# A decoder trunk layer on one core: two PSUM banks for attention scores and transposes, and branch gates kept as plain tanh

## The chip, the cores and the metric

The kernel runs on one core of a Trainium2 chip. A core has a matrix engine (TensorE, PE in the profile, with PEld for its weight loads), three engines for elementwise work (VectorE or DVE, ScalarE or ACT, GpSimd or POOL), a queue that mostly issues transfers (SyncE or SP), and 16 DMA engines. Matmul results land in PSUM, which has eight banks; ACT and DVE read them from there. Each engine works through its own instructions in order, and semaphores tie the engines together.

The metric is the device time of one execution in microseconds (us), lower is better. The kernel before was timed three times: 2133.55, 2133.91 and 2136.91 us, median 2133.91.

## What is computed

One inference step of one decoder layer, for a prompt of 1024 rows and 8 single-row samples, all in fp32, with a model width of 1024. In short:

```
h   = RMSNorm(x) * (1 + scale1) + shift1            # scale, shift, gate from silu(c) @ w_mod
z   = h @ w_in                                      # columns: delta rule, attention q k v, gates ga gb
y_a = GatedRMSNorm(GatedDeltaRule(conv4(q, k, v))) @ w_gdn_out
y_b = SlidingWindowSinkAttention(q, k, v) @ w_swa_out     # window 128, 16 heads, 4 key heads
x   = x + gate1 * (sigmoid(ga) * y_a + sigmoid(gb) * y_b) @ w_o
h2  = RMSNorm(x) * (1 + scale2) + shift2
x   = x + gate2 * (silu(conv3(h2 @ w_gate)) * (h2 @ w_up)) @ w_down
y   = RMSNorm(x)
```

Beside y the kernel returns the updated states: the delta rule's matrices, the last rows of both convolutions, and the last 128 keys and values.

## The kernel before, in words

**Matmuls.** Every projection multiplies split operands: a matrix is stored as a high part, rounded to the fast fp32r format, and a low part, the rest. `split` (L127) makes both: ACT copies to the high part (L129), DVE subtracts it from the source (L130). `mm3` (L177) adds three products, high x high, high x low, low x high (L180 to L182). The 1032 columns (rows of x) are worked on in three parts of 384, 384 and 264 (`PARTS`), or in four quarters of 256, 256, 260 and 260 (`QUARTERS`). A projection of one tile of 128 output channels over one part is 24 matmuls into one PSUM bank of the pool "mm", which an evacuation function then empties.

**Stages.** Setup: `modulation` (L250) computes the conditioning into tile "sc" and its transposes, `norm_part` (L278) spreads the row norms through "sc", `turn_part` (L304) transposes x through "pt" and "pv". Attention (L473): keys, queries and values are projected; four groups (one key head, four query heads) of eight blocks (128 queries) follow. Delta rule: eight heads are prepared, inverted and scanned in chunks. Branches (L1289): the two output projections with their gates. Then the output projection, the second norm, and the feed-forward part.

**An attention block** (L628). Two halves of two heads each: four matmuls write the scores into "sc" (L639, L640); ACT copies the older key block's scores to tile E (L643), DVE copies the newer block's where they are causal (L645). The softmax runs on E: row maximum on DVE (L647), exponentials with sums on ACT (L655), scaling by the reciprocal on ACT and DVE (L660, L662). PE transposes the four heads into "pt", DVE masks them on the way out (L667, L670), PE multiplies with the values into "pv" (L676, L678), ACT copies the result (L679).

**PSUM during setup and attention.** The pool q2 holds "sc", "pt" and "pv", beside two banks "mm" (pmm) and one more (pmf). How many buffers a tag has is decided in `t`, which keeps a table: the first number given for a pool and a tag stays (a `setdefault`). `modulation` and `conditioning` are the first to ask for "sc" and "pt" and name no number, which leaves the pool's own, one; `attention_block` asks later, with bufs=2. Before them, a line in `run` sets numbers for tags of the SBUF pool p2 only.

**The gates.** `gates` (L1266) is a generator that projects the 16 tiles of ga and gb. It serves as filler: other stages call it for a few matmuls at a time, and the branches run what is left. Its evacuation takes tanh(z / 2) on ACT (L1279), makes it a sigmoid on POOL, 0.5 * t + 0.5 (L1280), and stores it to DRAM from SP (L1281). The buffers are "mrows" during attention, two of "gt" during the delta rule, three of "sgx" in the branches. In `branches`, `yb_out` and `ya_out` evacuate the output projections: the stored gate is loaded again (L1351), multiplied with the bank on DVE (L1301, L1305), the two branches are added (L1306), and the sum is split into the operands "mix" (bmh, bml) of the next projection.

**The order of the work.** The program states the work in one order with priorities: `weave` interleaves generators, `later` moves a piece back, `issue_after` ties one to another. A planner then simulates the engines with its own costs and writes each engine's instructions in the order in which they could start there. That order is fixed when the chip runs it.

Of the kernel before, what the change touches and what calls it, by code (L numbers as in the profile page):

```python
# [9 lines left out]
F32 = mybir.dt.float32  # L10
F32R = mybir.dt.float32r
U32 = mybir.dt.uint32
AF = mybir.ActivationFunctionType
ALU = mybir.AluOpType
# [50 lines left out]
class Step:  # L65
# [1200 lines left out]
    def gates(self):  # L1266

        nc = self.nc
        self.sgb, self.sga = self.t(self.dr, [8, P, NT], "sgb"), self.t(self.dr, [8, P, NT], "sga")
        tiles = [(col + j * P, dst[j]) for col, dst in ((COL_GB, self.sgb), (COL_GA, self.sga)) for j in range(8)]  # L1270
        load = lambda i: self.win(tiles[i][0], where=self.fill_where[i % len(self.fill_where)])
        ahead = None
        for i, (col, dst) in enumerate(tiles):
            w, ahead = ahead or load(i), None

            def out(t, ps):
                lo, n = PARTS[t]
                s = self.t(self.gt[0], [P, 384], self.gt[1], bufs={"gt": 2, "sgx": 3}.get(self.gt[1]))[:, :n]
                nc.scalar.activation(s, ps, AF.Tanh, scale=0.5)  # L1279
                nc.gpsimd.tensor_scalar(s, s, 0.5, 0.5, op0=ALU.mult, op1=ALU.add)  # L1280
                nc.sync.dma_start(dst[:, lo:lo + n], s)  # L1281

            for t in range(3):
                for step in self.project_steps(w, self.h, out, (t,), self.fill_psum):
                    if self.ahead and ahead is None and i < 15:
                        ahead = load(i + 1)
                    yield

    def branches(self, pool, pool2):  # L1289
        nc, I = self.nc, self.I  # L1290
        ob = [self.load_part(pool2, self.ob, t) for t in range(3)]
        ub = [self.t(pool, [P, KC, n], f"t{t}", bufs=1) for t, (_, n) in enumerate(PARTS)]
        self.fill_where, self.gt, self.ahead, self.fill_psum = [self.where], (pool, "sgx"), True, None
        for _ in self.filler:
            pass
        samples = self.sample_delta()
        self.mm = [self.pmm, self.pmm, self.pso, self.pso]
        gate = lambda src, j, t: self.gate_part(pool, src[j][:, PARTS[t][0]:PARTS[t][0] + PARTS[t][1]], t)

        def yb_out(t, ps):  # L1300
            nc.vector.tensor_tensor(ub[t][:, j, :], ps, gate(self.sgb, j, t), op=ALU.mult)  # L1301

        def ya_out(t, ps):
            u, v = ub[t][:, j, :], gate(self.sga, j, t)
            nc.vector.tensor_tensor(v, ps, v, op=ALU.mult)  # L1305
            nc.vector.tensor_tensor(u, u, v, op=ALU.add)  # L1306
            r0, n = PARTS[t]
            for q, (lo, m) in enumerate(QUARTERS):
                c, e = max(lo, r0), min(lo + m, r0 + n)
                if c < e:  # L1310
                    self.split(*(x[:, j, c - lo:e - lo] for x in self.mix[q]), u[:, c - r0:e - r0])

        def load(name, j):
            raw = self.t(pool, [P, KC, P], "raw2", bufs=1) if j % 2 else None
            return self.load_w(I[name][0][:, j * P:(j + 1) * P], raw=raw)

        ahead = load("w_swa_out", 0)
        for j in range(6):
            w, ahead = ahead, load("w_swa_out", j + 1)
            for t in range(3):  # L1320
                if j or t == 2:
                    with self.tc.issue_after(self.last.ins):
                        next(samples, None)
                self.project(w, ob, yb_out, (t,))

        w = [ahead, load("w_swa_out", 7)]
        for _ in samples:
            pass
        oa = {}
        for t in range(3):  # L1330
            for j in (6, 7):
                self.project(w[j - 6], ob, yb_out, (t,))
            oa[t] = self.load_part(pool2, self.oa, t)
        self.bctx.close()
        self.bm = self.pool("bm", 1, side="right")
        self.mix = [tuple(self.t(self.bm, [P, KC, QW], f"bm{x}{q}", F32R)[:, :, :n] for x in "hl")
                    for q, (_, n) in enumerate(QUARTERS)]
        for j0 in (0, 2, 4, 6):
            w = [load("w_gdn_out", j) for j in (j0, j0 + 1)]
            if 0 < j0 < 6:  # L1340
                for j in (j0, j0 + 1):
                    self.project(w[j - j0], oa, ya_out)
                continue

            for t in range(3):
                for j in (j0, j0 + 1):
                    self.project(w[j - j0], oa, ya_out, (t,))
# [498 lines left out]
    def run(self):  # L1846
        S, nc = ExitStack, self.nc
        self.constants()
        with S() as ca:
            with S() as c:  # L1850
                pool, psum = self.pool("p2", 1, ctx=c), self.pool("q2", 1, PSUM, ctx=c)
                for tag, bufs in dict(qst=8, raw=2, kh=2, kl=2, E=3, obt=2, pp=2, pc=2, o=2).items():
                    self.bufs[id(pool), tag] = bufs
                self.conditioning(pool, psum)
                self.vectors(pool, psum)
                self.h = [self.new_part(t) for t in range(2)]
                vs = [self.t(self.b1, [P, 4, 384], f"b1{x}2") for x in "hl"]
                self.xT = self.t(self.dr, [KC, P, NT], "xT")
                self.a1 = self.const([P, KC, 9], "a1")
                rs, raws, self.stores, self.turned, self.chunks = {}, {}, [], [], []  # L1860
                w = []

                def part(t):
                    xs, rs[t] = self.norm_part(pool, psum, t, ["qst"] * 3 if t else ["raw", "raw", "qst"])
                    raws[t] = self.turn_part(pool, psum, t, xs, ROOMS[t])

                for lo in (8, 0, 12, 4):
                    self.modulation(pool, psum, "sc", lo, (("qst", 8),), "mrows")
                    if lo in (8, 12):
                        self.norm_scale(self.a1, 8, self.n1w, lo - 8, lo - 4)  # L1870
                    if lo in (8, 0):
                        part(lo == 0)
                        w.append(self.win((COL_SQ, COL_SK)[lo == 8]))
                    if lo == 0:
                        for t in range(2):
                            self.modulate(pool, t, range(4), raws[t], rs[t])
                    for t in range(2) if lo in (12, 4) else ():
                        for k in range(4, KC):
                            v = vs[t][:, k - 4, :]
                            if lo == 12:  # L1880
                                self.scale_tile(v, t, k, raws[t][k], rs[t])
                            else:
                                self.shift_tile(v, t, k)
                self.h.append(self.new_part(2))
                part(2)
                self.store_turned()
                self.modulate_samples(pool, 2, raws[2][KC], rs[2], self.a1, 0)
                self.modulate(pool, 2, range(KC), raws[2], rs[2])
                self.start = w
                self.attention(pool, psum)  # L1890
# [5 lines left out]
            with S() as c:  # L1896
                pa, pool, psum = self.pool("pa", 1, ctx=c), self.pool("p4", 1, ctx=c), self.pool("q4", 1, PSUM, ctx=c)
# [72 lines left out]
```

## Time and profile before

| what | value |
|---|---|
| median of three runs | 2133.91 us |
| the profiled execution's own time | 2135.05 us |
| its span (first to last instruction) | 2132.9 us |
| PE busy | 2065.0 us (97%) |
| DVE, ACT, POOL busy | 1330.2, 799.6, 311.6 us |
| setup, about | 0 to 75 us |
| attention, about | 75 to 412 us |
| delta rule, about | 412 to 1110 us |
| branches, about | 1110 to 1310 us |
| output projection, second norm, feed-forward | 1310 us to the end |

The profile is of one execution, with instructions in microseconds from the span's start. A group or a row names the line of the kernel, the engine, the operation, and "out<-in" by the names of the tiles. "Idle before" is the time in which the engine stood still just before an instruction, and "<-" names what ended it. Matmuls are pipelined, and their recorded ends are modelled: several are in flight at a time, so a busy PE is not always a PE at its best. PEclk, or the granted clock, is the share of full speed that PE was allowed in a stretch. Idle time of an engine that doesn't set the end costs nothing.

### The profile page before, as it was taken

The page shows a single profiled execution, that of the slowest core. Times are in us where ns is not written, and L with a number is a line of the kernel's source. Part 1 is how long each engine was busy: PE and PEld are TensorE (multiplying, and loading weights), DVE is VectorE, ACT ScalarE, POOL GpSimd, SP SyncE. Part 2 cuts the span into 40 slices and gives each one's busy share as a digit, 9 for nine tenths or more (in the row PEclk, how much of TensorE's full clock was granted, in tenths as well). Part 3 has the DMA queues.
Part 4 walks back from the last instruction along what each step waited for, and adds up shares of the span by engine and source line. Part 5 has one row for each costly group of instructions (what it writes and reads, how often), then busy time and mean ns, then how long its engine had stood idle before and what let it go on. Part 6 is the DMA issues. An engine that isn't in the chain of part 4 may idle for free.

```text
span 2132.9 us, 41264 instructions
## 1 busy us (share of the span) xinstructions
PE 2065.0 (97%) x16515; PEld 1951.9 (92%) x16515; DVE 1330.2 (62%) x2887; ACT 799.6 (37%) x2094; POOL 311.6 (15%) x436
## 2 busy tenths in 40 slices
PE   7998999999899999999999999999999999999998
PEld 3886877899898999999999999999999999999998
DVE  6656676474574676775144654578767767765565
ACT  5545555333333334433332422353334334421102
POOL 3100000120221111112120000003332332100000
PEclk9999999999999999999999999999999999999999
DMA  9434322341322232122257836223322222353202
GB/s 334 135 110 143 103 87 85 101 105 43 91 64 79 49 82 60 51 64 67 77 184 202 268 91 193 61 65 102 100 71 80 89 72 77 127 225 109 70 3 81
DMA packets 257946, 223.91 MB, mean 105 GB/s; under 512 B 57586, under 2 KB 224277, under 8 KB 257738
## 3 DMA queue, kind: packets, MB, share of 16 engines
q1 hardware_dynamic: 254714, 212.50, 32.7%
q0 software_dynamic: 1568, 4.95, 0.7%
q10 hardware_dynamic: 1472, 3.82, 0.5%
q8 instruction: 130, 2.13, 0.4%
q14 instruction: 62, 0.51, 0.1%
HBM read 171.25 MB, written 52.33 MB: 105 GB/s over the span
## 4 chain that ended last, share of the span: by engine, by line
PE 62%; DVE 5%; DMA 3%; ACT 2%; issue 1%; SPq 1%; POOL 0%; DVEq 0%; POOLq 0%; ACTq 0%
PE mm L180 14%; PE mm L181 14%; PE mm L182 14%; PE wv L181 3%; PE wv L180 3%; PE wv L182 3%; PE wy L182 2%; PE wy L180 2%; PE wy L181 2%; DMA b1l<-dlr 1%; PE rc L947 1%; DMA raw<-in_w_o_dram 1%; PE rc L944 1%; PE rc L951 1%; DVE w L130 1%
## 5 line engine op out<-in xcount | busy, mean ns | idle before, releaser
L180 PE MATMUL mm<-b1h,wh 128*128 128x384 f32 (+1 forms) x1440 | 471.8, 329 | 6.0 <-ACT gt L1279 1.9
L182 PE MATMUL mm<-b1h,wl 128*128 128x384 f32 (+1 forms) x1440 | 466.1, 325 | 0.9 <-DVE wl L130 0.8
L181 PE MATMUL mm<-b1l,wh 128*128 128x384 f32 (+1 forms) x1440 | 465.7, 324 | 0.9 <-DVE b1l L130 0.9
L180 PEld LDWEIGHTS mm<-b1h,wh 128*128 128x128 f32 x1440 | 271.8, 189 | 15.1 <-issue 5.5
L181 PEld LDWEIGHTS mm<-b1l,wh 128*128 128x128 f32 x1440 | 272.2, 189 | 5.8 <-issue 4.1
L182 PEld LDWEIGHTS mm<-b1h,wl 128*128 128x128 f32 x1440 | 271.7, 189 | 6.0 <-issue 3.9
L180 PE MATMUL mm<-pk,w 128*128 128x260 f32 (+1 forms) x440 | 124.5, 283 | 1.4 <-ACT r L1588 0.8
L181 PE MATMUL mm<-pk,w 128*128 128x260 f32 (+1 forms) x440 | 124.2, 282 | 0.8 <-DVE pk L130 0.8
L129 ACT ACTIVATE wh<-raw 128x1024 fp32r<-128x1024 f32 x77 | 80.9, 1050 | 116.4 <-PE mm L181 90.8
L182 PE MATMUL mm<-pk,w 128*128 128x260 f32 (+1 forms) x440 | 124.1, 283 | 0.3 <-DVE w L130 0.3
L130 DVE TENSOR_TENSOR wl<-raw,wh 128x1024 fp32r<-128x1024 f32 x76 | 92.9, 1223 | 49.3 <-ACT wh L129 47.9
L180 PE MATMUL mm<-b2h,wh 128*128 128x384 f32 (+1 forms) x384 | 122.6, 320 | 0.8 <-ACT wh L129 0.8
L181 PE MATMUL mm<-b2l,wh 128*128 128x384 f32 (+1 forms) x384 | 121.9, 318 | 0.0
L182 PE MATMUL mm<-b2h,wl 128*128 128x384 f32 (+1 forms) x384 | 121.2, 318 | 0.3 <-DVE wl L130 0.3
L180 PE MATMUL mm<-bmh,pk 128*128 128x260 f32 (+1 forms) x380 | 110.7, 291 | 2.0 <-ACT pk L129 2.0
L182 PE MATMUL mm<-bmh,pk 128*128 128x256 f32 (+1 forms) x380 | 110.3, 290 | 1.3 <-DVE pk L130 1.3
L1432 DVE SCALAR_TENSOR_TENSOR x<-mm,mT,x 128x256 f32<-128x256 f32 (+2 forms) x133 | 63.5, 481 | 74.9 <-PE mm L182 74.5
L181 PE MATMUL mm<-bml,pk 128*128 128x260 f32 (+1 forms) x353 | 102.0, 289 | 0.0
L180 PE MATMUL mm<-bmh,w 128*128 128x260 f32 (+1 forms) x320 | 92.0, 287 | 0.0
L182 PE MATMUL mm<-bmh,w 128*128 128x260 f32 (+1 forms) x320 | 91.3, 285 | 0.0
L130 DVE TENSOR_TENSOR w<-ws,w 128x512 fp32r<-128x512 f32 x88 | 60.2, 685 | 41.6 <-ACT w L129 41.6
L180 PEld LDWEIGHTS mm<-pk,w 128*128 128x128 f32 x440 | 82.7, 188 | 2.0 <-ACT r L1588 1.0
(609 smaller groups left out, 5659.1 us busy)
## 6 DMA issues: line engine op xcount, KB each, us to landing
raw<-in_w_in_dram SPq DMA_DIRECT2D x60, 512.0 KB
bml<-act SPq DMA_DIRECT2D x22, 516.0 KB
raw<-in_w_ffn_gate_dram SPq DMA_DIRECT2D x22, 512.0 KB
raw<-in_w_ffn_up_dram SPq DMA_DIRECT2D x22, 512.0 KB
raw<-in_w_ffn_down_dram SPq DMA_DIRECT2D x22, 512.0 KB
qst<-in_w_mod_dram SPq DMA_DIRECT2D x16, 512.0 KB
raw<-in_w_mod_dram SPq DMA_DIRECT2D x16, 512.0 KB
act<-fa SPq DMA_DIRECT2D x22, 260.0 KB
```

Source lines behind the costliest of these rows:

```text
L129: self.nc.scalar.activation(hi, x, AF.Copy)
L130: (eng or self.nc.vector).tensor_tensor(lo, x, hi.bitcast(F32), op=ALU.subtract)
L180: mm(ps, whi, xhi, start=first, stop=False, **kw)
L181: mm(ps, whi, xlo, start=False, stop=False, **kw)
L182: self.last = mm(ps, wlo, xhi, start=False, stop=last, **kw)
L944: yield step(nc.tensor.matmul(ks, K[:, n, :], S, start=True, stop=True))
L947: yield step(nc.tensor.matmul(sp, W[:, n, :], y, start=True, stop=True))
L951: yield step(nc.tensor.matmul(ds, kd[:, n, :], s, start=True, stop=True))
L1432: nc.vector.scalar_tensor_tensor(x[:, :np_], ps[:, :np_], self.mT[:, m + j, 8:9], x[:, :np_], op0=ALU.mult, op1=ALU.add)
```

## The change

Two edits. First, the tags "pt" and "sc" of the pool q2 are entered in the table with two buffers each, ahead of the first tile. With "mm" (2), pmf (1) and "pv" (1) that makes eight banks. It holds for the modulation and the transposes of the setup as well as for the attention blocks; the tiles, the instructions that use them and the order of the program stay. The planner makes its order anew.

Second, the pass on POOL (L1280) is gone, and what is stored is tanh(z / 2). A sigmoid is half of tanh plus one, so the branches take (gate + 1) * bank in one scalar_tensor_tensor on DVE, in place of gate * bank. The sum of the branches is then twice the sum wanted, and the factor 0.5 goes into the split: ACT's copy to the high part scales by 0.5, and DVE computes 0.5 * sum minus the high part, a scalar_tensor_tensor in place of a tensor_tensor.

```diff
@@ gates, out(t, ps)
                 nc.scalar.activation(s, ps, AF.Tanh, scale=0.5)
-                nc.gpsimd.tensor_scalar(s, s, 0.5, 0.5, op0=ALU.mult, op1=ALU.add)
                 nc.sync.dma_start(dst[:, lo:lo + n], s)
@@ branches
         def yb_out(t, ps):
-            nc.vector.tensor_tensor(ub[t][:, j, :], ps, gate(self.sgb, j, t), op=ALU.mult)
+            nc.vector.scalar_tensor_tensor(ub[t][:, j, :], gate(self.sgb, j, t), 1.0, ps, op0=ALU.add, op1=ALU.mult)
 
         def ya_out(t, ps):
             u, v = ub[t][:, j, :], gate(self.sga, j, t)
-            nc.vector.tensor_tensor(v, ps, v, op=ALU.mult)
+            nc.vector.scalar_tensor_tensor(v, v, 1.0, ps, op0=ALU.add, op1=ALU.mult)
             nc.vector.tensor_tensor(u, u, v, op=ALU.add)
...
                 if c < e:
-                    self.split(*(x[:, j, c - lo:e - lo] for x in self.mix[q]), u[:, c - r0:e - r0])
+                    hi, low = (x[:, j, c - lo:e - lo] for x in self.mix[q])
+                    part = u[:, c - r0:e - r0]
+                    nc.scalar.activation(hi, part, AF.Copy, scale=0.5)
+                    nc.vector.scalar_tensor_tensor(low, part, 0.5, hi.bitcast(F32), op0=ALU.mult, op1=ALU.subtract)
@@ run
                     self.bufs[id(pool), tag] = bufs
+                for tag, bufs in dict(pt=2,sc=2).items():
+                    self.bufs[id(psum), tag] = bufs
                 self.conditioning(pool, psum)
```

## The prediction

> **What bounds the kernel now.** I read the page first, for the engine that has no room.
>
> ```profile
> span 2132.9 us, 41264 instructions
> PE 2065.0 (97%) x16515; PEld 1951.9 (92%) x16515; DVE 1330.2 (62%) x2887; ACT 799.6 (37%) x2094; POOL 311.6 (15%) x436
> ```
>
> TensorE (PE) is busy for 2065.0 of 2132.9 us. No matmul is added or removed, so whatever the change gains must come out of the other 67.9 us, or out of time in which the granted clock was low. Next I read busy time by stage (columns: length, then busy PE, PEld, DVE, ACT, POOL, then granted clock, DMA share, GB/s): setup, attention, delta rule, branches.
>
> ```profile
> 0.00:75.00 75.00, 56.20 (x304) 37.27 (x305) 50.25 (x111) 42.01 (x84) 20.39 (x48) 0.90 0.89 306
> 75.00:412.00 337.00, 326.41 (x2124) 267.61 (x2124) 206.97 (x572) 165.61 (x562) 17.62 (x43) 0.98 0.30 95
> 412.00:1110.00 698.00, 676.10 (x6033) 650.27 (x6032) 403.10 (x877) 252.31 (x781) 129.02 (x195) 1.00 0.29 78
> 1110.00:1310.00 200.00, 196.87 (x1372) 194.68 (x1370) 109.87 (x247) 64.95 (x151) 12.83 (x15) 0.99 0.64 191
> ```
>
> In attention, where the extra banks serve, PE idles 337.00 - 326.41 = 10.6 us. That, and the clock, is the purse. Slices of 25 us (same columns) show where it lies:
>
> ```profile
> 175.00:200.00 25.00, 19.54 (x131) 14.08 (x132) 17.87 (x66) 13.86 (x58) 0.00 (x0) 0.86 0.38 134
> ...
> 250.00:275.00 25.00, 22.47 (x147) 19.28 (x145) 19.48 (x70) 13.59 (x47) 0.00 (x0) 1.00 0.14 44
> 275.00:300.00 25.00, 24.82 (x157) 17.04 (x157) 15.64 (x51) 13.27 (x55) 0.20 (x2) 0.94 0.32 110
> 300.00:325.00 25.00, 24.77 (x163) 22.40 (x162) 22.20 (x47) 14.20 (x44) 4.29 (x10) 1.00 0.48 150
> ```
>
> 5.5 us of the idle time are in 175 to 200 and 2.5 us in 250 to 275, the places where blocks of attention run with few projection matmuls between them. Elsewhere projections fill the waits: at 300 to 325 PE idles 0.2 us.
>
> **The second bank for scores and for transposes.** An attention block (L628) computes scores in two halves of four matmuls (L639, L640) into tile "sc". The text asks for two buffers, but the pool's table keeps the number it is given first for a tag, and setup asks first and gives none; so "sc" and "pt" each have one bank. The trace shows that it is so. In the timeline (start, length, instruction, in brackets the idle time before it and its releaser):
>
> ```profile
> 271.00 0.28 PE L640 MATMUL sc<-kl,qst 128*128 128x256 f32 x1
> ...
> 272.72 0.36 ACT L643 ACTIVATE E<-sc 128x256 f32<-128x256 f32 x1
> ...
> 273.14 0.42 DVE L645 COPY_PREDICATED E<-trilu,sc 128x256 f32<-128x256 uint32 x1
> ...
> 273.61 0.39 PE L639 MATMUL sc<-kh,qst 128*128 128x256 f32 x1 [1.45 <-DVE E L645]
> ```
>
> The half written at 271.00 is read by ACT (L643) and then by DVE (L645), and the next half's first matmul starts at 273.61, when L645 has finished: 1.45 us idle for a bank. The groups of the attention stage sum such waits (busy us, mean ns, then idle before and its releasers):
>
> ```profile
> L639 PE MATMUL sc<-kh,qst 128*128 128x256 f32 (+1 forms) x126 | 37.1, 314 | 3.9 <-DVE E L645 2.7 <-DVE m L648 0.6 <-DVE den L656 0.5
> ...
> L189 PE MATMUL pt<-ident,E 128*128 128x128 f32 x128 | 22.0, 281 | 1.7 <-DVE den L656 0.9 <-ACT E L660 0.8
> ...
> L189 PE MATMUL pt<-ident,vch 128*128 128x128 f32 x16 | 2.8, 307 | 0.3 <-DVE V L547 0.3
> ```
>
> I count as the bank's own: all 3.9 us before L639 (its two inputs, keys and queries, come from projections, and every releaser is DVE, the bank's last reader; L648 and L656 stand just behind L645 in DVE's order), and 0.3 us before the transposes of the values. With two banks a half waits for the half before the last, long evicted: **-4.2 us**. The 1.7 us before the transposes of E are waits for their input, not for a bank; two banks don't remove them. What is late next is the softmax chain. Six of the idle places in the worst slice:
>
> ```profile
> 175.53 0.40 PE L639 MATMUL sc<-kh,qst 128*128 128x256 f32 x1 [0.54 <-DVE den L656]
> ...
> 177.40 1.19 PE L189 MATMUL pt<-ident,E 128*128 128x128 f32 x4 [0.82 <-ACT E L660]
> ...
> 185.18 0.63 PE L189 MATMUL pt<-ident,E 128*128 128x128 f32 x4 [0.88 <-DVE den L656]
> ...
> 189.84 0.64 PE L189 MATMUL mm<-ident,vch 24*128 24x24 f32 x8 [0.97 <-DMA vch<-in_state_gdn_conv_dram]
> ...
> 192.78 0.64 PE L189 MATMUL mm<-ident,vch 24*128 24x24 f32 x8 [0.61 <-DMA vch<-in_state_gdn_conv_dram]
> ...
> 194.48 0.62 PE L263 MATMUL mm<-wmh,cTr 128*32 128x512 f32 x2 [1.06 <-DVE den L657]
> ```
>
> Only 0.54 us here is for the bank; 2.76 us wait for softmax results and 1.58 us for a load. Scores that come earlier also start the softmax earlier, so these could shrink; the lower bound of that is 0, the upper bound is all idle time of the stage, 10.6 us. I take 0 beyond the 4.2 us, because the chain's own engines aren't idle there (DVE 17.87 of 25 us).
>
> **The clock.** In 175 to 200 the granted clock is 0.86 and in 275 to 300 it is 0.94, each beside idle time of PE: 25 x 0.14 + 25 x 0.06 = 3.5 + 1.5 = 5.0 us of full clock lost. Bounds 0 and 5.0. The second dip follows the bank wait at 273.61, the first follows softmax and load waits, so I take the second alone: **-1.5 us**.
>
> The Trainium skill ("TensorE: Matmul & The Clock Gate", Part 1: The HAM clock gate) says that the clock halves after an idle window of about 3.4 us, and warns of gaps longer than that. By that rule none of the gaps shown, at most 1.45 us, would cost clock, and this term would be 0, the sum -6.6 us. This trace doesn't bear it out read as a limit on a single gap: the clock fell to 0.86 with gaps of 0.54 to 1.06 us.
>
> **Setup.** The same tags serve the turning of x. Idle here is 75 - 56.2 = 18.8 us, but DMA is 0.89 busy over the stage, so most of it is loads.
>
> ```profile
> 62.25 0.48 ACT L321 COPY raw<-pt 128x384 f32<-128x384 f32 x1
> ...
> 62.79 0.80 PE L189 MATMUL pt<-ident,qst 8*128 8x8 f32 x8 [1.96 <-ACT raw L321]
> ```
>
> The sample rows' transposes waited 1.96 us until the one "pt" bank was copied out. The bound is 0 to 2.0 us; I take half, **-1.0 us**, since the samples' next steps run on DVE, which is 50.25 of 75 us busy.
>
> **Gates as plain tanh.** L1280, one GpSimd (POOL) pass per stored part of a gate, goes away (tile view: count, then min/median/max ns):
>
> ```profile
> L1280 POOL TENSOR_SCALAR gt<-gt x42: 401/512/1470, 469.4 to 1115.0; 128x384 f32<-128x384 f32 x28, 128x264 f32<-128x264 f32 x14
> ...
> L1280 POOL TENSOR_SCALAR mrows<-mrows x6: 413/512/1171, 361.5 to 408.9; 128x384 f32<-128x384 f32 x4, 128x264 f32<-128x264 f32 x2
> ```
>
> 48 x 0.51 = 25 us of POOL, which is 15% busy: worth nothing by itself, since PE works on projections meanwhile. What it can hold up is the store behind it: two "gt" buffers, so the next tanh waits for the store and keeps a projection's bank.
>
> ```profile
> 540.43 1.84 POOL L1280 TENSOR_SCALAR gt<-gt 128x264 f32<-128x264 f32 x2
> ...
> 540.90 5.76 SPq L1281 DMA_DIRECT2D sgb<-gt  x3
> ...
> 545.09 0.49 ACT L1279 ACTIVATE gt<-mm 128x384 f32<-128x384 f32 x1 [1.99 <-DMA sgb<-gt]
> ...
> 545.63 0.39 PE L180 MATMUL mm<-b1h,wh 128*128 128x264 f32 x1 [1.42 <-ACT gt L1279]
> ```
>
> POOL came late to the gate (it was copying blocks for the inverse), SP's queue stood at the store, ACT waited 1.99 us and PE 1.42 us. Without L1280 the store follows ACT: **-1.4 us**, once; bounds 0 and 2.0 (ACT's wait). SP's queue, which also issues weight loads, is freed about 0.5 us earlier each time; costed at nothing because the loads run ahead.
>
> The added arithmetic: L1301 and L1305 become scalar_tensor_tensor, the split's high part gets a scale on ACT, its low part becomes scalar_tensor_tensor. Rows of both forms at the same width:
>
> ```profile
> L1301 DVE TENSOR_TENSOR t<-mm,sgx 128x384 f32<-128x384 f32 x16 | 8.9, 555 | 22.0 <-PE mm L182 20.0 <-DMA sgx<-sgb 1.9
> ...
> L857 DVE SCALAR_TENSOR_TENSOR sg<-th,mm 128x384 f32<-128x384 f32 x16 | 8.4, 549 | 15.0 <-DMA oa<-sg 8.8 <-ACT th L856 6.2
> ...
> L130 DVE TENSOR_TENSOR bml<-t,bmh 128x256 fp32r<-128x256 f32 x16 | 6.8, 425 | 3.5 <-ACT bmh L129 3.4
> ...
> L590 DVE SCALAR_TENSOR_TENSOR qst<-mm,qst 64x384 fp32r<-64x384 f32 x32 | 17.8, 555 | 11.5 <-ACT qst L589 10.4
> L590 DVE SCALAR_TENSOR_TENSOR qst<-mm,qst 64x256 fp32r<-64x256 f32 x16 | 6.8, 423 | 1.8 <-ACT qst L589 1.3
> ```
>
> L857 is the very form (tanh + 1) x bank: 549 against 555 ns. L590 at 256 columns, 423 against 425 ns, stands for the low part. So **0**, hidden under PE anyway (196.87 of 200 us busy in the branches). If the new form cost 50 ns more, 96 instructions would be 4.8 us of DVE, which has 90 us free there.
>
> **Sum.** -4.2 - 1.5 - 1.0 - 1.4 = -8.1 us. The profiled execution took 2135.05 us (its span plus 2.15), so 2126.95; it lay 1.14 us above the median of the three runs, 2133.91, so on that footing 2125.8, rounded to **2126**, 0.4% faster.
>
> **Rivals.** *The wait only moves* (0.23): as in 175 to 200, the softmax chain or a load stands right behind the bank, and PE, busy by order of the queue, gets back only the gap at 545.63 and about a quarter of the 4.2 us: 2.5 us less, 2131. For it: five of the six rows of the worst slice. Against: at 273.61 the bank stands alone. *The whole chain loosens* (0.15): all 10.6 us, 5.0 us of clock, 2.0 of setup and 1.4 of the gate, -19.0, 2115. For it: a block's halves no longer follow each other through ACT and DVE, so every softmax starts sooner. Against: DVE at 22.20 of 25 us in 300 to 325. *DVE becomes the bound, slower* (0.17): the planner puts instructions in order by its own simulated times, and with two banks the score halves, which come earlier in the program, are evicted ahead of the projections' evictions (L590). DVE is in order; the 32 + 16 L590 are two to a query part, 24 parts. If each part's bank is freed later by one more eviction of scores (0.42 us as at 273.14), PE, with two projection banks, waits up to 24 x 0.42 = 10 us; less the 4.2 us that is +6 us, 2140. It decides once DVE is above about 22 of 25 us in more slices than the one shown. *That nothing happens* because the number of buffers isn't taken up is excluded: the new lines set the table before the first tile is asked for, and 2 + 1 projection banks, 2 + 2 and 1 for "pv" are the eight.
>
> **How the numbers follow.** The forecast has 0.45, the loosened chain 0.15, together 0.60 faster. By over 0.2% means by over 4.3 us, about what a measurement of this kernel can tell from no change. The moved wait is the 0.23 within that, the DVE bound the 0.17 slower. The range reaches down to the loosened chain, 2114, and up to just short of the slow rival's price, 2139; past both ends lies some 0.2.
>
> **What would show it.** In the changed profile: before L639 almost no idle time released by DVE; scores of a second half starting before L645 of the first; the slices around 175 and 275 with more PE busy time, and a clock of 1.00 in 275 to 300; no POOL at the gates and no wait of ACT for sgb's store at about 545; the span from 1310 to the end unchanged at 823 us. I am wrong if the attention stage is no shorter, if idle time before L639 turns into as much before L180 released by DVE L590, or if the delta-rule stage, where only POOL's gates go, changes by more than 3 us either way.

## The result, and the profile after

The changed kernel takes 2123.22 us (median of 6 runs, 2115.26 to 2128.92) beside 2133.82 us for the kernel before (6 runs on the same chip). The ratio is 0.9944, with a 95% interval of 0.9923 to 0.9964. The gain is 10.6 us; 7.9 had been forecast. The profiled execution took 2123.98 us. The head of its page:

```profile
span 2122.2 us, 41192 instructions
PE 2056.5 (97%) x16515; PEld 1951.4 (92%) x16515; DVE 1326.9 (63%) x2887; ACT 797.7 (38%) x2094; POOL 280.7 (13%) x388
```

The span is 10.7 us shorter, but PE's idle time fell only from 67.9 to 65.7 us. Most of the gain stood as *busy* time before. To see where, I cut both spans at the same pieces of work: at the first transpose of a head's values in the delta rule (the first mark), and at the first matmul of the branches. The number of matmuls in each stretch (in brackets behind PE's busy time) shows that the work is equal, but for two or three matmuls. The kernel before, by stretches (columns: length, busy PE, PEld, DVE, ACT, POOL, clock, DMA share, GB/s):

```profile
0.00:448.90 448.90, 417.60 (x2657) 339.50 (x2658) 282.06 (x718) 222.26 (x695) 44.14 (x99) 0.97 0.42 138
448.90:1108.50 659.60, 639.60 (x5794) 614.15 (x5793) 376.76 (x838) 236.38 (x731) 122.88 (x186) 1.00 0.27 71
1108.50:2132.90 1024.40, 1007.83 (x8069) 998.28 (x8067) 671.38 (x1332) 340.97 (x670) 144.62 (x151) 0.99 0.36 112
```

The changed kernel, by the same work:

```profile
0.00:434.40 434.40, 405.26 (x2659) 334.77 (x2660) 281.65 (x723) 220.66 (x696) 40.21 (x94) 0.98 0.43 143
434.40:1098.10 663.70, 645.35 (x5792) 620.09 (x5790) 374.45 (x834) 236.40 (x729) 96.04 (x144) 0.99 0.26 71
1098.10:2122.20 1024.10, 1005.87 (x8069) 996.57 (x8067) 670.84 (x1332) 340.64 (x670) 144.42 (x150) 0.99 0.36 112
```

Setup and attention gain 14.5 us, the delta rule gives 4.1 back, and the rest takes as long as before. Of the 14.5 us only 31.3 - 29.1 = 2.2 are idle time. The trace's record of the clock has 27.3 us at half speed in the first stretch before and 13.7 after, so 6.8 us less are lost to it. The remaining 5.5 us are neither, and stood as busy time. They fit short waits that the profile counts as work: a score matmul is recorded with 0.28 us although the next one can begin 0.11 or 0.12 us later, so a wait of up to some 0.16 us leaves no idle time. Timeline of the changed kernel (start, length):

```profile
267.81 0.28 PE L640 MATMUL sc<-kl,qst 128*128 128x256 f32 x1
267.92 0.28 PE L639 MATMUL sc<-kh,qst 128*128 128x256 f32 x1
268.04 0.28 PE L640 MATMUL sc<-kl,qst 128*128 128x256 f32 x1
```

The slices of 25 us that were thin before, now:

```profile
175.00:200.00 25.00, 25.00 (x173) 17.61 (x172) 17.54 (x57) 15.98 (x64) 0.00 (x0) 1.00 0.50 162
250.00:275.00 25.00, 25.00 (x179) 18.27 (x178) 19.87 (x65) 16.17 (x70) 0.20 (x2) 1.00 0.25 85
275.00:300.00 25.00, 25.00 (x165) 20.88 (x163) 20.18 (x42) 14.20 (x42) 3.47 (x8) 1.00 0.28 88
300.00:325.00 25.00, 23.33 (x161) 21.91 (x160) 11.49 (x36) 13.65 (x48) 2.41 (x6) 1.00 0.41 131
```

From 175 to 200 PE now does 173 matmuls instead of 131, without idle time and at full clock. The groups of PE up to the first mark, of the kernel before (busy us, mean ns, then idle before them and its releasers):

```profile
L180 PE MATMUL mm<-b1h,wh 128*128 128x384 f32 (+1 forms) x473 | 154.3, 330 | 2.2 <-ACT b1h L129 1.3 <-DVE kl L567 0.4 <-DVE qst L590 0.2
...
L639 PE MATMUL sc<-kh,qst 128*128 128x256 f32 (+1 forms) x128 | 37.6, 314 | 4.0 <-DVE E L645 2.7 <-DVE m L648 0.6 <-DVE den L656 0.5
L676 PE MATMUL pv<-pc,V 128*64 128x256 f32 x128 | 35.5, 421 | 0.6 <-DVE pc L667 0.5
L189 PE MATMUL pt<-ident,E 128*128 128x128 f32 x128 | 22.0, 281 | 1.7 <-DVE den L656 0.9 <-ACT E L660 0.8
L189 PE MATMUL tp<-ident,K 128*128 128x128 f32 x8 | 1.1, 276 | 1.9 <-DMA K<-kqv 1.9
```

and of the changed kernel:

```profile
L180 PE MATMUL mm<-b1h,wh 128*128 128x384 f32 (+1 forms) x474 | 155.1, 330 | 3.6 <-DVE kl L567 2.8 <-ACT wh L129 0.4 <-DVE obs L771 0.2
L639 PE MATMUL sc<-kh,qst 128*128 128x256 f32 (+1 forms) x128 | 34.2, 296 | 0.3 <-DVE E L645 0.3
L676 PE MATMUL pv<-pc,V 128*64 128x256 f32 x128 | 31.1, 404 | 1.4 <-DVE pc L667 1.4
L189 PE MATMUL pt<-ident,E 128*128 128x128 f32 x128 | 24.1, 281 | 3.5 <-ACT E L660 3.5
L189 PE MATMUL tp<-ident,K 128*128 128x128 f32 x8 | 1.9, 424 | 3.7 <-DMA K<-kqv 3.7
```

The wait for the score bank is gone, 4.0 to 0.3 us. A good part of it stands elsewhere now: 1.8 us more before the transposes of E, 1.8 more before the first transposes of keys, 0.8 before the values, and 2.4 more before projections that wait for an eviction of the key projections in DVE's order (L567). In the changed kernel's timeline, the largest gap of three of them:

```profile
62.27 0.41 PE L180 MATMUL mm<-b1h,wh 128*128 128x384 f32 x1 [2.67 <-DVE kl L567]
...
344.56 0.62 PE L189 MATMUL pt<-ident,E 128*128 128x128 f32 x2 [2.25 <-ACT E L660]
...
408.41 1.94 PE L189 MATMUL tp<-ident,K 128*128 128x128 f32 x8 [3.75 <-DMA K<-kqv]
```

### The profile page after: what moved, and what is told of

The parts are those of the page before. It is cut to its first block, busy times and chain, and to the rows that moved or that the text cites. A ratio compares the mean times of both kernels' runs of the same rounds, so it can differ in the third digit from the quotient of the medians.

```text
span 2122.2 us, 41192 instructions
## 1 busy us (share of the span) xinstructions
PE 2056.5 (97%) x16515; PEld 1951.4 (92%) x16515; DVE 1326.9 (63%) x2887; ACT 797.7 (38%) x2094; POOL 280.7 (13%) x388
## 4 chain that ended last, share of the span: by engine, by line
PE 84%; DVE 7%; DMA 4%; ACT 3%; issue 1%; SPq 1%; POOL 0%; ACTq 0%; DVEq 0%; POOLq 0%
PE mm L180 19%; PE mm L182 19%; PE mm L181 19%; PE wv L181 3%; PE wv L182 3%; PE wv L180 3%; PE wy L182 2%; PE wy L180 2%; PE wy L181 2%; PE pt L189 1%; PE pv L678 1%; DMA b1l<-dlr 1%; PE mm L263 1%; PE pv L676 1%; DVE wl L130 1%
## 5 line engine op out<-in xcount | busy, mean ns | idle before, releaser
L180 PE MATMUL mm<-b1h,wh 128*128 128x384 f32 (+1 forms) x1440 | 474.5, 331 | 7.4 <-DVE kl L567 2.8
L180 PEld LDWEIGHTS mm<-b1h,wh 128*128 128x128 f32 x1440 | 273.0, 190 | 19.0 <-issue 9.9
L180 PE MATMUL mm<-pk,w 128*128 128x260 f32 (+1 forms) x440 | 124.4, 283 | 0.6 <-ACT pk L129 0.6
L180 PE MATMUL mm<-b2h,wh 128*128 128x384 f32 (+1 forms) x384 | 122.3, 319 | 1.9 <-ACT wh L129 1.9
L180 PE MATMUL mm<-bmh,pk 128*128 128x260 f32 (+1 forms) x380 | 110.5, 291 | 3.2 <-ACT pk L129 2.3
L180 PE MATMUL mm<-bmh,w 128*128 128x260 f32 (+1 forms) x320 | 91.2, 285 | 0.2 <-DVE fa L1667 0.2
```

The source lines that it names most:

```text
L180: mm(ps, whi, xhi, start=first, stop=False, **kw)
```

## The experiments

All runs of the table were timed beside the kernel before on the same chip. "Lost clock" is the mean over the runs of span x (1 - granted clock), and "at full clock" is the span less that; the kernel before has 23.8 and 2110.5 us beside e1 to e4 (29 runs), 22.8 and 2109.3 beside e5 to e8 (23), 25.1 and 2109.4 beside e9 to e11 (13), and 24.0 and 2106.4 beside e12 (7). These four groups ran on four chips, so rows of different groups are compared by their ratios, or by how far each lies from its own kernel before. (For the runs of the kernel before beside the change, the clocks are not on record.) Runs of one kernel scatter by about 2 us at full clock, and their times go with the clock, mostly 1 to 2 us per 0.001.

| kernel | median us | ratio, 95% interval | lost clock | at full clock |
|---|---|---|---|---|
| the change | 2123.22 | 0.9944, 0.9923 to 0.9964 | 21.6 | 2099.4 |
| e1 banks alone | 2126.01 | 0.9953, 0.9940 to 0.9966 | 23.4 | 2100.8 |
| e2 gates alone | 2134.22 | 0.9990, 0.9978 to 1.0002 | 24.7 | 2108.1 |
| e3 gates, second bank for scores | 2130.65 | 0.9967, 0.9953 to 0.9980 | 27.8 | 2100.1 |
| e4 gates, second bank for transposes | 2131.87 | 0.9984, 0.9973 to 0.9994 | 21.9 | 2108.4 |
| e5 two names, attention only | 2113.87 | 0.9903, 0.9885 to 0.9921 | 17.2 | 2094.0 |
| e6 early load of keys | 2121.72 | 0.9941, 0.9926 to 0.9956 | 20.8 | 2099.3 |
| e7 three banks for scores | 2124.40 | 0.9962, 0.9948 to 0.9976 | 19.8 | 2104.5 |
| e8 gates' POOL pass twice | 2135.81 | 1.0005, 0.9992 to 1.0018 | 25.1 | 2108.8 |
| e9 two names, setup only | 2129.78 | 0.9969, 0.9955 to 0.9984 | 21.8 | 2106.6 |
| e10 two names, setup and attention | 2113.81 | 0.9898, 0.9882 to 0.9915 | 16.1 | 2096.4 |
| e11 two names, scores in attention only | 2127.41 | 0.9957, 0.9941 to 0.9973 | 27.6 | 2098.2 |
| e12 two names for scores, one for transposes | 2109.81 | 0.9893, 0.9876 to 0.9909 | 14.8 | 2093.7 |

### Which part of the change gains

**e1, the banks alone**, in the kernel before:

```diff
+                for tag, bufs in dict(pt=2,sc=2).items():
+                    self.bufs[id(psum), tag] = bufs
                 self.conditioning(pool, psum)
```

> The two edits apart: both second banks, the gates as before with their POOL pass. If the banks carry the gain (the forecast's view: 6.7 of its 8.1 us, scaled to the 10.6 us measured), this is 8 to 10 us faster than before, 2124 to 2126 us. If the gates' store carries it, or if the gain is no more than the planner's new order, it lies within 4 us of before.

**e2, the gates alone**: the changed kernel without those two lines.

> The gates alone: plain tanh and the scaling where used, one bank each for scores and transposes. The forecast's term is -1.4 us, at most -2: within 2 us of before, 2132 to 2134 us. The rival that POOL's passes held up the delta rule more widely (they sit between its own POOL steps) gives 4 us or more faster. If it is slower by 2 us or more, the changed order in itself costs time.

**e3 and e4, one of the two second banks**, in the changed kernel:

```diff
-                for tag, bufs in dict(pt=2,sc=2).items():
+                for tag, bufs in dict(sc=2).items():      # e3;   e4: dict(pt=2)
```

> The whole change but for the second bank of the transposes (pt has one, sc two). The forecast gives the scores 3.9 us of idle time and 1.5 us of clock, and the gate 1.4 us: 6 to 7 us faster than before, about 2127 us. If the transposes' bank matters as much, it is under 4 us faster.

> The whole change but for the second bank of the scores (sc has one, pt two). The forecast gives the transposes 0.3 us in attention and 1.0 us in setup, and the gate 1.4 us: 2 to 3 us faster than before, about 2131 us. If transposes that wait behind masks in DVE's order are what holds the blocks apart, it is 6 us or more faster.

The banks alone give 2136.53 - 2126.01 = 10.5 us, the gates 2.3 with an interval that reaches past no change, so the gain is the banks'. Of the two second banks, taken one at a time, it is the scores' that gains: at full clock e3 is 8.0 us below e2, e4 is where e2 is. By the time, e3 shows less of that (3.6 us below e2) because it loses 3.1 us more to the clock. What the transposes' bank adds to the scores' is told with e11. The groups tell the same. The first line is of the gates alone, the second of e3, the third of e4:

```profile
L639 PE MATMUL sc<-kh,qst 128*128 128x256 f32 (+1 forms) x128 | 37.4, 313 | 4.1 <-DVE E L645 2.7 <-DVE m L648 0.7 <-DVE den L656 0.5
```

```profile
L639 PE MATMUL sc<-kh,qst 128*128 128x256 f32 (+1 forms) x128 | 33.9, 295 | 0.1
```

```profile
L639 PE MATMUL sc<-kh,qst 128*128 128x256 f32 (+1 forms) x128 | 37.1, 310 | 3.4 <-DVE E L645 2.3 <-DVE m L652 0.6 <-DVE den L656 0.5
```

**e7, three banks for the scores**, none more for the transposes (`dict(sc=3)`):

> The change with three banks for scores and one for transposes. If two banks already take the scores' wait away (in the changed kernel 0.3 us are left before L639), the third is worth nothing and this equals the kernel with two banks for scores and one for transposes, 0.9967 of before (0.995 to 0.998). If scores still wait for banks out of sight, inside what counts as busy, it is 2 us or more faster than that.

The ratio is 0.9962, against 0.9967 with two, as expected of a third bank that is worth nothing. At full clock it is no better: 4.8 us below its own kernel before, where e3 is 10.4 below. Its median is lower by the clock, of which it loses 3.0 us less than its kernel before, and e3 4.0 more.

### What the gates' pass cost

**e8, the pass on POOL done twice** in the kernel before; the second pass completes the sigmoid.

```diff
-                nc.gpsimd.tensor_scalar(s, s, 0.5, 0.5, op0=ALU.mult, op1=ALU.add)
+                nc.gpsimd.tensor_scalar(s, s, 1.0, 1.0, op0=ALU.mult, op1=ALU.add)
+                nc.gpsimd.tensor_scalar(s, s, 0.5, 0.0, op0=ALU.mult, op1=ALU.add)
```

> The kernel before, with the gates' pass on POOL done twice (times one plus one, then times a half): 48 passes of some 0.5 us more, 25 us of POOL. If POOL's passes hold up the delta rule in proportion, as the 0.1% of the gates alone suggests, it is 2 to 3 us slower than before. If the forecast is right that one late store is all, it is 0 to 1.5 us slower.

1.0005, with an interval around 1: a second pass costs nothing that can be measured. PE's wait for the gate, 1.42 us at 545.63 before, is 1.20 us here, at 543.63, so the longer pass didn't lengthen it. What leaving the pass out does to that wait is told under the gates' term below.

### What is late next

**e6, the first head's keys and queries of the delta rule loaded from POOL's queue**, in the changed kernel, so that the load doesn't stand behind SP's other transfers:

```diff
-                self.nc.sync.dma_start(out.rearrange("p n i -> p (n i)"), self.kqv0[i])
+                (self.nc.gpsimd if i < 2 else self.nc.sync).dma_start(out.rearrange("p n i -> p (n i)"), self.kqv0[i])
```

> The whole change, and the two loads of head 0's keys and queries for the delta rule issued by POOL in place of SP, where they stand behind a store and weight loads. In the changed kernel PE waits 3.75 us for that load at 408 and gets half the clock for 3.4 us after it. If the load can start earlier, 2 to 5 us faster than the change, 2119 to 2121 us beside its 2123. If it waits for memory of the attention stage or for the store of the same data and not for SP's queue, no difference (within 2 us).

The load now goes out at 395.22, and the transposes find their keys there:

```profile
410.57 1.03 PE L189 MATMUL tp<-ident,K 128*128 128x128 f32 x8
```

The 3.75 us of idle time before them are gone, and the time is the same: 0.9941 against 0.9944. So a wait that can be seen on PE was worth nothing that can be measured here. The clock gained nothing either: the record has 6.8 us at half speed from 416.3 on, where the changed kernel has 3.4 from 407.9. Where the 3.75 us went in the planner's new order was not followed.

### The same banks under two names

The planner takes a tile's bank from those of its tag. With one tag and two buffers a score half may get either; with two tags of one buffer, used in turn, each half has its own. **e5** does so in the attention only (setup has one bank each), in the changed kernel; **e11** for the scores alone:

```diff
-            sc = self.t(psum, [P, 2, 256], "sc", bufs=2)
+            sc = self.t(psum, [P, 2, 256], ("sc", "sc2")[half])
-        pt = self.t(psum, [P, 4, P], "pt", bufs=2)
+        pt = self.t(psum, [P, 4, P], ("pt", "pt2")[n % 2])      # e11: "pt"
-                for tag, bufs in dict(pt=2,sc=2).items():
-                    self.bufs[id(psum), tag] = bufs
```

> The whole change, but with the second banks used in the attention blocks alone: scores and transposes alternate there between two tags of one bank each, while setup has one bank for each as before. If setup's second banks are worth what the forecast gave them, 1.0 us (at most 2), this is 8 to 11 us faster than before, as the change itself is. If setup carries several us, it is under 7 us faster. If setup's reordering costs time (the changed kernel has a new gap of 2.67 us at 62), it is faster than the change by 1 to 3 us.

> Second bank for the scores in the attention blocks alone; transposes and all of setup have one bank each; gates as in the change. If the scores carry the gain, it is 0.993 of before or better, within 5 us of the run that doubles both in attention. If the transposes' second bank is needed too, it is 0.995 to 0.997, as the run with two banks for scores in setup and attention was.

e5 came out faster than the change itself, by 0.0041 with the intervals apart; its expectation had allowed for 1 to 3 us, and this is 8.7. e11 is 0.9957, so the second branch of its expectation came true: the transposes' second bank is needed too. e5 has that bank more and is 0.0054 lower, intervals apart. The traces say the same without the clock. The table has the length up to the first mark, less half of the time at half speed there, from one profile of each kernel:

| banks in attention: scores, transposes | kernels | us |
|---|---|---|
| 1, 1 | before, e2, e8, e9 | 435.0 to 435.9 |
| 1, 2 | e4 | 437.0 |
| 2 (e7: 3), 1 | e3, e7, e11 | 430.8 to 430.9 |
| 2, 2 | the change, e1, e5, e10, e12 | 424.1 to 427.5 |

(e6 does some 35 matmuls more before that mark and is left out.) By itself the transposes' second bank gives nothing; beside the scores' it gives 3 to 7 us there. **e9** puts the alternation into `t`, for the setup only, with one bank each in attention; **e10** for both stages:

```diff
@@ t
+        if tag in self.flip:
+            self.flip[tag] ^= 1
+            tag += "2" * self.flip[tag]
@@ run
-                for tag, bufs in dict(pt=2,sc=2).items():
-                    self.bufs[id(psum), tag] = bufs
+                self.flip = dict(sc=1, pt=1)
...
+                self.flip = {}      # e9: before attention; e10: after it
```

> The opposite of the run with second banks in attention alone: setup has two banks for scores and transposes (two tags of one bank in turn), the attention blocks have one each. If setup's second banks cost the 9 us by which the change lies behind that run, this is slower than the gates alone (0.999 of before): 1.002 to 1.004 of before, 2138 us or more. If they do no harm by themselves, it equals the gates alone within 2 us; if they gain what the forecast gave them, it is 1 to 2 us faster than the gates alone.

> The change with two tags of one bank taken in turn, in setup and in attention, in place of one tag with two buffers. The same banks are double, so if it is the banks that count this equals the change, 0.9944 of before (0.992 to 0.997). If the alternation by name is what makes the run with attention alone fast, this is 0.99 of before or better.

**e12** gives two names to the scores only; the transposes keep one name with two buffers:

```diff
-                self.flip = dict(sc=1, pt=1)
+                self.bufs[id(psum), "pt"] = 2
+                self.flip = dict(sc=1)
```

> The changed kernel with one difference: the two banks of the scores are two names of one buffer each, used in turn, while the transposes' two banks stay one name with two buffers. Both names in turn gave 0.990 and 2113.8 us, one name with two buffers for both 0.994 and about 2122. Theory one, the scores' naming makes the difference, since it fixes which half waits for which: 0.990, about 2114, and at the start of a group the first halves of blocks 0 to 3 stand ahead of the second halves on PE. Theory two, the transposes' naming makes it: 0.994, about 2122, with scores in the order of the changed kernel. Theory three, the gain of both names is that run's order and its clock and belongs to neither: anything between 0.988 and 0.997, with the time that is lost to the granted clock moving along with it, some 1 to 2 us per 0.001 of clock.

e9 lies 0.0021 below the gates alone, 4.5 us, for the setup's second banks; the intervals overlap a little, so it could be anything from nothing to some 9 us. By the means it is clock: at full clock e9 lies 2.8 us below its kernel before, and e2 2.4. e10 has the same banks as the change and is 0.9898 against 0.9944, intervals apart. e12 is as fast as e10, 0.9893, with intervals that overlap: of the two pairs of names it is the scores' that counts, not the transposes'. Against the change it is 0.0051 lower, 10.9 us. The means beside it lie 5.7 us lower at full clock and 6.8 us lower in lost clock. Of the 5.7 up to 4 can be the chip's, whose kernel before is that much shorter at full clock too. The two profiles have 8.1 and 5.5 us. So both have a share, and its size isn't settled.

PE's order of instructions at the start of the first group of blocks shows what the names do. S0a is the first half of block 0's scores, T0 its transposes, V0 its products with the values; in brackets other matmuls of the program ahead. A half stands twice where scores of another block come between its two heads:

```
before    (230)S0a (120)S0b (24)S1a (52)S1b (30)S2a (15)T0 (7)S2b (13)V0 T1
change    (278)S0a (48)S0b S1a (24)S0b S1b (24)S2a S2b (54)S3a S3b (18)T0 (19)T1
e10, e12  (278)S0a (24)S1a (24)S0b S2a (24)S0b S3a (24)S1b (54)S2b (23)T0 (3)S3b (12)T1
```

Before, the transposes of a block come between the scores of the next ones. With two buffers of one name, four blocks of scores run ahead. With two names the first halves of four blocks run ahead and the second halves follow. e12 by the same work as above (in its own line numbers, which lie 3 higher: L642 is the L639 of the others):

```profile
0.00:429.60 429.60, 405.90 (x2656) 334.06 (x2657) 278.89 (x718) 220.91 (x695) 40.39 (x93) 0.99 0.43 144
429.60:1089.20 659.60, 643.27 (x5794) 618.25 (x5792) 375.19 (x838) 236.74 (x731) 98.80 (x145) 0.99 0.26 71
1089.20:2108.50 1019.30, 1002.71 (x8069) 994.44 (x8067) 671.43 (x1332) 340.36 (x670) 144.67 (x150) 0.99 0.35 113
```

```profile
L642 PE MATMUL sc<-kh,qst 128*128 128x256 f32 (+1 forms) x128 | 35.6, 302 | 0.2 <-DVE E L648 0.2
L192 PE MATMUL pt<-ident,E 128*128 128x128 f32 x128 | 23.8, 281 | 0.9 <-ACT E L663 0.9
```

Against the changed kernel it gains 4.8 us up to the first mark, where the wait before the transposes of E is 0.9 instead of 3.5 us; 4.1 in the delta rule; and 4.8 behind it, where the names serve nothing and only the planner's order and the clock differ. That the names of the scores' banks set the order is shown, and that the three kernels with two names and both second banks (e5, e10, e12) are the fastest. That the names by themselves bring the time is not: in the table above, e1 has one name and 425.4 us, against 424.1 to 425.7 with two, so up to the first mark the names are worth from nothing to 3 us, and e11 has two names and 0.9957. The rest is the clock and the order in the later stages, as the third theory had it; why this order is the better one there isn't settled.

## Why the prediction was right, and where not

The sum, -8.1 us, stands beside -10.6 measured. That they lie so near is in part luck: setup and attention gained 14.5 us, where the sum had 6.7, and the delta rule lost 4.1, where the sum had a gain of 1.4. Its terms:

**The second banks, -4.2.** The place and the cause were right: the idle time before L639 fell by 3.7 us, e3 against e4 shows that the scores' bank removes it, and second halves now start before L645 of the first half (four blocks of scores ahead of the first transposes). The size was not. Errors of mine partly cancel. I gave the transposes' bank 0.3 us, and beside the scores' it is worth 3 to 7. I counted only waits that show as idle time, while 5.5 us more were won out of what the profile calls busy. And I took 0 for what is late next: the idle time before the transposes of E doubled, 1.7 to 3.5 us, and the load of the keys went from 1.9 to 3.7. The rival that the wait only moves was half right: of the idle time that can be seen only 2.2 us were won.

**The clock, -1.5, bounds 0 and 5.0.** The mean over all runs is 21.6 us lost, and the kernel before has 22.8 to 25.1, so 1 to 3 us less. The place was wrong: I expected one dip less at 275. Both dips went (clock 1.00 in both slices), setup lost less too, 6.8 us in all, and as much came back in the delta rule. I also read the first dip too loosely. In the record it runs from 175.8 to 182.6, so of the six gaps that I listed only the first, 0.54 us, lies before it. By the rule of the Trainium skill ("TensorE: Matmul & The Clock Gate", Part 1: The HAM clock gate), read as a limit of 3.4 us on a single gap, the term would have been 0. The dips at 175 and 275 stood beside gaps of at most 1.45 us and went with them, so the trace goes against that reading. Where one gap is that long it agrees: right behind the 3.75 us before the keys there is a dip, from 407.9 to 411.3, and those eight transposes take 424 instead of 276 ns.

**The delta rule.** I had said that I would be wrong if it changed by more than 3 us. It grew by 4.1. The trace of the changed kernel has 13.7 us at half clock there, 6.8 us lost, before it had none. Two of the dips, and the gap beside the second (columns as above):

```profile
500.00:525.00 25.00, 23.21 (x155) 22.79 (x154) 14.80 (x33) 4.68 (x17) 8.09 (x8) 0.93 0.34 82
525.00:550.00 25.00, 23.30 (x204) 21.29 (x202) 15.48 (x46) 7.42 (x20) 2.22 (x3) 1.00 0.25 68
550.00:575.00 25.00, 23.53 (x272) 21.56 (x262) 6.76 (x14) 8.78 (x29) 1.30 (x2) 0.86 0.21 68
```

```profile
558.15 0.69 PE L180 MATMUL mm<-b1h,wh 128*128 128x384 f32 x1 [1.47 <-ACT gt L1279]
```

Over thirteen kernels (e6 divides its work otherwise) the length of this stretch goes, if roughly, with its time at half clock in the record: none 659.6 (before) and 656.8 (e10); 3.4 us 657.3 to 659.6 (e4, e5, e9); 6.8 us 659.5 (e2); 10.2 us 659.6 (e12) and 662.6 (e8); 13.7 us 660.9 to 663.7 (e3, e7, the change); 23.9 us 669.9 (e1); 27.3 us 668.3 (e11). Less the lost clock, the changed kernel takes 656.9 us, which is shorter than before. That the clock is the cause is read from this and not from an experiment that sets the clock alone.

**Setup, -1.0.** e9 against e2 says -4.5, with the wide bounds told above, and at full clock only -0.4. PE's wait of 1.96 us at 62.79 went, and one of 2.67 us came at 62.27. What the changed kernel gains is earlier work and clock: in the first 75 us of the changed kernel 337 matmuls run instead of 304, at 0.93 instead of 0.90.

```profile
0.00:75.00 75.00, 57.16 (x337) 40.96 (x338) 53.30 (x116) 43.41 (x89) 21.50 (x50) 0.93 0.88 312
```

**Gates, -1.4.** The mechanism held, but the changed kernel doesn't show it. With the gates alone (e2) ACT no longer waits for the store at this place, and PE waits 0.41 us instead of 1.42:

```profile
545.24 0.39 PE L180 MATMUL mm<-b1h,wh 128*128 128x264 f32 x1 [0.41 <-ACT gt L1279]
```

Behind the gates' tanh the delta rule's projections idle 0.6 us in e2 and 1.9 before: 1.3 us, the size of the term. In the changed kernel the tanh doesn't stand behind a store either. But another stall is at 558.15, 1.47 us before a projection that waits for the tanh's eviction of its bank, because ACT comes to the tanh only after four copies of W and a weight split:

```profile
555.05 1.68 ACT L1045 COPY W<-T 32x256 f32<-32x256 f32 x4 [3.33 <-DVE T L1041]
556.76 1.06 ACT L129 ACTIVATE wh<-raw 128x1024 fp32r<-128x1024 f32 x1
557.72 0.37 ACT L1279 ACTIVATE gt<-mm 128x264 f32<-128x264 f32 x1
```

So the idle time behind the gates' tanh is 2.3 us there. The group of the changed kernel's delta rule:

```profile
L180 PE MATMUL mm<-b1h,wh 128*128 128x384 f32 (+1 forms) x967 | 319.6, 331 | 3.8 <-ACT gt L1279 2.3 <-DVE sg L857 1.3
```

The same 1.47 us stands in e3, e4, e6, e7 and e11, and not in e2, e5, e9, e10 and e12, which store the same gates. So it comes with the order that the planner made, and not with the gates. Whether the whole time gains the 2.3 us that e2's median shows, or nothing, is within its interval and stays open.

**The added arithmetic, 0.** Right. The branches of the changed kernel, by form:

```profile
L1304 DVE SCALAR_TENSOR_TENSOR sgx<-sgx,mm 128x384 f32<-128x384 f32 x16 | 8.9, 554 | 23.0 <-PE mm L182 23.0
L1300 DVE SCALAR_TENSOR_TENSOR t<-sgx,mm 128x384 f32<-128x384 f32 x16 | 8.8, 551 | 22.5 <-PE mm L182 20.5 <-DMA sgx<-sgb 2.0
L1313 DVE SCALAR_TENSOR_TENSOR bml<-t,bmh 128x256 fp32r<-128x256 f32 x16 | 7.1, 446 | 3.5 <-ACT bmh L1312 3.4
```

551 and 554 ns for the gated products, against 555 before. The low part takes 446 instead of 425 ns at 256 columns, which is 0.3 us of DVE over its 16 pieces; DVE waits there for PE and ACT anyway.

**The rivals.** DVE did not become the bound: up to the first mark no idle time before L180 stands against L590 among the three largest releasers any more (0.2 us before). The whole chain did not loosen either in the changed kernel, but e10 and e12 come near the 2115 us that this rival gave: with the scores' banks named in turn, e12 idles 23.7 us up to the first mark instead of 29.1, at a higher clock. The stage behind the branches' start, which the prediction held for unchanged, is: 1024.4 and 1024.1 us.

## What to carry to other kernels

Where PE is nearly always busy, the idle time before a group doesn't tell what its wait is worth. It can be more: up to the first mark 2.2 us of idle time went and 14.5 us were won. It can be nothing: the 3.75 us that e6 removed. So compare two kernels by the time between equal pieces of work. A second bank frees the order more than it removes one wait, and one that gives nothing by itself, like the transposes', can pay beside another. How it is handed out (one name with two buffers, or two names in turn) can go with as much again, 0.9944 against 0.9893 here, though a part of that is clock. Look at the granted clock stage by stage, since a gain in one stage can be lost to it in the next.

## What was not expected of the hardware

The clock is lost in whole pieces: in the record every dip ahead of a span's last few us lasts 3.4 or 6.8 us at half speed, and one 10.2 (e11); 3.4 and 6.8 make 0.93 and 0.86 of 25 us. The dips also stand on a grid. In each of the fourteen traces they start whole multiples of 3.41 us apart (before: 18.8, 29.0, 63.1, 73.4, 175.8 and 274.8, which are 3, 10, 3, 30 and 29 steps), and where the grid lies against the span's start differs from trace to trace. How much PE idles in a stretch doesn't tell whether it is lost. e10 idles more than e12 in the same 25 us, and keeps its clock (first line e10, second e12):

```profile
525.00:550.00 25.00, 21.68 (x242) 19.74 (x243) 13.94 (x41) 6.35 (x19) 2.23 (x3) 1.00 0.23 62
```

```profile
525.00:550.00 25.00, 22.71 (x205) 20.89 (x207) 12.30 (x36) 5.40 (x16) 1.60 (x2) 0.86 0.22 60
```

Nor does the one step of the grid ahead of a dip tell. In e12 PE is busy for 2.85 of the 3.4 us from 551.9, and the clock halves at 555.3; in e10 it is busy for 1.94 of the 3.4 us from 529.2, and the clock stays. So it isn't the busy time of the profile alone that decides.

The same program also differs from run to run: the six runs of the change have a clock of 0.988 to 0.993 and times of 2128.92 to 2115.26 us. The Trainium skill ("TensorE: Matmul & The Clock Gate", Part 1, What's actually happening) says that the window in which activity is judged runs freely, and doesn't begin with the kernel; that agrees with the grid and with these differences. By what a step is judged no run here shows.
